# The state's update behind the 64-join, and decays, AH and X tied behind level copies, in the second DeltaNet pass of a diffusion step

## The chip, the cores and the metric

The kernel runs on one core of one Trainium2 chip. The metric is device time in microseconds (us) of one execution. The engines are named as in the profile: PE (TensorE, matmuls), DVE (VectorE), ACT (ScalarE), POOL (GpSimd) and SP (SyncE, which here only issues DMAs). A change of under 0.3% can't be told from none with this kernel.

## The reference

One layer of a hybrid backbone is run on 128 context tokens and 2048 latent tokens of width 1024, in float32. The token stream is normalised and modulated, projected once, and goes through two parallel groups of heads (a gated DeltaNet that is scanned in both directions, and a gated spatial MLP); their outputs are projected, added, and go through a squared-ReLU MLP. What matters here is the DeltaNet, cut to its core:

```python
a_mat = where(strict, einsum(k_beta, k) * decay, 0)          # per chunk and head
sol = triangular_solve(a_mat + eye, [v * beta, k_beta * exp(g)])
u, w = sol[..., :DV], sol[..., DV:]
qk = einsum(q, k) * decay
def step(S, xs):
    v_new = u_c - w_c @ S
    o = qd @ S + qk_c @ v_new
    S = S * exp(gl) + kd.T @ v_new
    return S, o
```

So every chunk needs a decay matrix, the inverse of a unit triangular matrix, and a step of a recurrent state S (4 heads of 128 x 128).

## The kernel before

The program has three stages. First come the projections, the convolution and the norms for 17 tiles of 128 tokens (one of context, sixteen latent). Then come the two DeltaNet passes, the first in the forward direction with the gated MLP as fill work, the second in the backward direction with the gating, the output projection w_out and the operands of the MLP as fill work. Then comes the MLP.

In the passes, a tile in one direction is a **unit**: units 0 to 16 are the forward pass (`d` is 0), units 17 to 33 the backward pass (`d` is 1, `NT` is 17). A unit has 17 **prep** steps that need no state and 4 **scan** steps that do. The prep steps, numbered from 0:

- 0: the decays. ACT makes `E` with four activations and one exponential (L1052, L1053), POOL masks it twice into `Es` and `E` (L1055, L1057).
- 1: DVE multiplies `KK` by beta and `Es`, one instruction per head (L1067); POOL sets the diagonal (L1071); ACT copies to f16 `AH` (L1074); DVE masks that into `X` (L1075).
- 2: PE transposes `X` (L1081), ACT copies `Y` (L1083), DVE makes the remainder `AL` (L1084).
- 3 to 12: the inverse, doubled in block size at levels 2, 4, 8, 16 and 32. Each level has two steps: PE multiplies `AH` and `Y` (L1101) and DVE masks the product into `P` (L1105); PE multiplies `P` and `X` twice (L1114, L1116) and ACT copies the new `Y` and `X` (L1117, L1118). At level 2 DVE also multiplies `QK` by `E` (L1121).
- 13 and 14: the **64-join**, the last doubling. Its first step is L1133 on PE and a copy `P` on ACT (L1134); its second is L1140 and L1142 on PE, a copy into `Y` on DVE (L1143) and one into `X` on ACT (L1144).
- 15 and 16: one Newton correction. PE multiplies `AH` and `AL` with `Y` (L1150, L1151), DVE makes `R` (L1153); PE multiplies `X` and `R`, ACT scales into `T` (L1162).

The scan steps: 0, the state times `kT` and `qT`; 1, `T` times `vt`, from which DVE makes `vs` (L1187) and ACT `vn` (L1189); 2, the **state's update**, eight f32 matmuls of `vs` and `kt` (L1026, `pd<-vs,kt`; an f32 product of a head shows as two) and four DVE instructions (L1201); 3, `QK` times `vn` and the output.

**The order of the work.** Every step gets a planned time in units of one period (one unit per period). With the second pass's figures (`WINDOWS`, from its ninth on), prep step j of unit n stands at n - 2.63 + (j + 0.5) * 2.57 / 17 and scan step j at n - 0.18 + (j + 0.5) * 1.18 / 4. While unit i is scanned, units i+1, i+2 and i+3 are in preparation. Fill work has times too: the eight w_out steps of a tile, of six matmuls each, are 0.125 apart (0.5975 and 0.7225 of a period are two of them), and a transpose stands at 0.5933. Steps are issued in the order of these times. A fill step is also bound on PE behind the first matmul of the fourth-last chain or prep step issued before it (`LAG3` is 3; `hist`).

A planner in the framework (`schedule_with_timeline_sim=True`) then makes the order of each engine from the order of issue: it runs a model of the engines and brings forward what it takes to be ready when an engine would be idle. On the chip each engine runs its list in order. A dependency added by `add_manual_dep` with `NoSync` puts no wait into the program; it only forbids the planner to place an instruction ahead of another one on the same engine.

`level_done` marks the last instruction of a step as urgent: the masks `P` of the levels on DVE and the copies `X` of the levels on ACT. `calm(f, lag)` issues `f` and binds each of its DVE and ACT instructions behind the last urgent one of its engine, or behind the one `lag` places further back. Before the change `calm` is used on the `KK` products of the second pass (lag 1), on one addition of the output projection (L1395) and on the steps that make the MLP's operands (L903, L904, L909).

Of the kernel before, what the change touches and what calls it, by code (L numbers as in the profile page):

```python
# [12 lines left out]
AF = mybir.ActivationFunctionType  # L13
ALU = mybir.AluOpType
# [7 lines left out]
NT = 17  # L22
NTOK = NT * P
H = 4
# [40 lines left out]
def hybrid_step(  # L65
# [7 lines left out]
    V, A, G, T = nc.vector, nc.scalar, nc.gpsimd, nc.tensor  # L73
# [74 lines left out]
    def bc4(ap):  # L148
        return ap.unsqueeze(1).to_broadcast([P, 4, P])
# [810 lines left out]
    with ExitStack() as ph:  # L960
# [41 lines left out]
        def level_done(n):  # L1002

            x = tc.nc.cur_bb.bb.instructions[-1]
            urgent[x.engine].append(x)

        def calm(f, lag=0):

            start = here()
            f()  # L1010
            for x in tc.nc.cur_bb.bb.instructions[start:]:
                if x.engine in urgent and len(urgent[x.engine]) > lag:
                    tc.add_manual_dep(x, urgent[x.engine][-1 - lag].name, mybir.DependencyInfo(
                        mybir.DependencyClass.NoSync, mybir.DependencyReason.DATA), reason="order")

        def unit(t, d):

            u = {}
            sg = 1 if d == 0 else -1

            def col(tab, h):
                return tab[:, t, d * 4 + h : d * 4 + h + 1]
# [25 lines left out]
            @prep.append  # L1048
            def _():
                e = s32("E")  # L1050
                for h in range(H):
                    A.activation(e[:, h, :], u["gb"][:, h, :], AF.Abs, scale=-1.0, bias=col(gcol, h))  # L1052
                A.activation(e, e, AF.Exp, scale=-1.0)  # L1053
                es = s32("Es")
                G.affine_select(out=es, in_=e, pattern=[[0, 4], [-sg, P]], compare_op=ALU.is_gt, fill=0.0,  # L1055
                                base=0, channel_multiplier=sg)
                G.affine_select(out=e, in_=e, pattern=[[0, 4], [sg, P]], compare_op=ALU.is_ge, fill=0.0,  # L1057
                                base=0, channel_multiplier=-sg)
                u["Es"], u["E"] = es, e

            @prep.append
            def _():
                a = u["KK"]

                def decayed():
                    for h in range(H):
                        V.scalar_tensor_tensor(out=a[:, h, :], in0=a[:, h, :], scalar=col(beta, h),  # L1067
                                               in1=u["Es"][:, h, :], op0=ALU.mult, op1=ALU.mult)

                calm(decayed, 1) if d else decayed()  # L1070
                G.affine_select(out=a, in_=a, pattern=[[0, 4], [1, P]], compare_op=ALU.not_equal, fill=1.0,  # L1071
                                base=0, channel_multiplier=-1)
                u["AH"], u["AL"], u["X"] = f16("AH", BA), f16("AL", BA), f16("X", BX)
                A.copy(u["AH"], a)  # L1074
                V.tensor_tensor(out=u["X"], in0=u["AH"], in1=bc4(bd2), op=ALU.mult)  # L1075

            @prep.append
            def _():
# [57 lines left out]
            @prep.append  # L1136
            def _():
                p = pd()
                for h in range(H):
                    T.matmul(p[:, h, 0:64], u["X"][:, h, :], pms[64][:, h, rb], start=True, stop=True)  # L1140
                for h in range(H):
                    T.matmul(p[:, h, 64:P], pms[64][:, h, :], u["X"][:, h, ra], start=True, stop=True)  # L1142
                V.tensor_copy(u["Y"][ra, :, rb], p[ra, :, 0:64])  # L1143
                A.copy(u["X"][rb, :, ra], p[rb, :, 64:P])  # L1144

            @prep.append
# [44 lines left out]
            @scan.append  # L1191
            def _():
                s = u["s"]
                p = pd()
                quad(p, u["kt"], u["vs"])
                sn = q32("S", 2)
                if s is None:
                    A.copy(sn, p)
                else:
                    for h in range(H):  # L1200
                        V.scalar_tensor_tensor(out=sn[:, h, :], in0=s[:, h, :], scalar=col(egl, h),  # L1201
                                               in1=p[:, h, :], op0=ALU.mult, op1=ALU.add)
                u["sn"] = sn

            @scan.append
# [205 lines left out]
        def at(time, fn, kind=None):  # L1411
            events.append((time, len(events), fn, kind))

        def spread(t0, t1, steps, kind):
            for j, st in enumerate(steps):
                at(t0 + (t1 - t0) * (j + 0.5) / len(steps), st, kind)

        def scan_step(i, f):
            def g():
                u = units[i]  # L1420
                if "s" not in u:
                    u["s"] = None if i in (0, NT) else units[i - 1]["sn"] if i not in (1, NT + 1) else u["s0"]
                f()
            return g
# [26 lines left out]
        for i, u in enumerate(units):  # L1451
            w = p2 if i <= NT else p3
            at(i - 3 if i > 1 else -12.1, lambda i=i, u=u: noted(("kk", i), u["prep_loads"]))
            at(i - 3 if i > 1 else -11.1, lambda i=i, u=u: after_weights(
                u["qk_load"], (("kk", 1),) if i < 2 else (), (mybir.EngineType.SP,)))
            at(i - 1, lambda i=i, u=u: after_weights(u["scan_loads"], LATER.get(i, ()), (mybir.EngineType.SP,)))
            u["prep"][:2] = [lambda i=i, f=f: after_weights(f, AHEAD_OF.get(i, ()), (mybir.EngineType.Activation,
                                                                                    mybir.EngineType.DVE))
                             for f in u["prep"][:2]]
            n = len(u["prep"])  # L1460
            for j, st in enumerate(u["prep"]):
                at(i - w[0] + (j + 0.5) * (w[0] - w[1]) / n if i or j > 9 else -11.6 if j < 2
                   else 0.2 * j - 8.15, st, "prep")
            spread(i + w[2], i + w[3], [scan_step(i, f) for f in u["scan"]], "chain")
            if i in (0, NT):
                at(i - 1, lambda i=i: state_load(i))
                at(i + w[2] + (w[3] - w[2]) * 0.7, lambda i=i: after(i))
            if i >= NT:
                at(i, lambda u=u: o_loads(u))
                first, second = o_steps(u)  # L1470
                spread(i + p3[4], i + p3[5], first, "fill")
                spread(i + p3[6], i + p3[7], second, "fill")
                if u["t"] > 8:
                    st = h2_steps(u["t"], pj, fraw, w512, fpart, fhalf, lambda u=u: u["x2"])
                    spread(i + p3[8], i + p3[9] + 0.2, st[:5], "fill")
                    spread(i + p3[9] + 0.2, i + p3[9] + 2.1, [lambda f=f: calm(f) for f in st[5:]], None)
# [620 lines left out]
```

## Time and profile before

| | us |
|---|---|
| median of three runs | 2576.61 |
| lowest, highest | 2570.27, 2578.84 |
| the profiled execution | 2574.76 |
| its span, first to last instruction | 2573.0 |
| first DeltaNet pass in the trace, about | 440 to 870 |
| second DeltaNet pass in the trace, about | 870 to 1222 |

The prediction shows rows of three kinds. A row of the **windows** view has the stretch (us from the span's start), its length, and the busy time of PE, of PE's weight loads, of DVE, ACT and POOL, each with the number of instructions in brackets; then the granted PE clock (1.00 is full), the DMA engines' busy share and GB/s. A row of the **waits** view reads: engine, tile and line that waited, the instruction that released it; the total in us, the number of times, the longest. A row of the **timeline** has the start and the length in us, the engine, the line, the operation, out<-in, the shape and the number of instructions merged; in square brackets stands the engine's idle time just before and what released it. Instructions of DVE and ACT that follow each other overlap in these records by a tenth of a microsecond or so, so the time one takes is read from the start of the next.

### The profile page before, as it was taken

The numbers are of one execution on the slowest core, as the hardware profiler recorded it, in microseconds if no ns is written. First come the engines' busy times: TensorE is split into PE (matmuls) and PEld (weight loads), VectorE is DVE, ScalarE is ACT, GpSimd is POOL, SyncE is SP. The second block draws the span as 40 slices with busy tenths as digits, with TensorE's granted clock in tenths as the row PEclk, the third lists the DMA queues.
The fourth block names the chain that finished last, engine by engine and source line by source line (L and its number), as shares of the span: only waits on it lengthen the run. The fifth ranks groups of instructions, "written<-read, shape, count | busy, mean of one in ns | idle before, by whom it ended". The sixth has DMA issues, their size and how long they took to land.

```text
span 2573.0 us, 44472 instructions
## 1 busy us (share of the span) xinstructions
PE 2536.3 (99%) x15268; PEld 2136.7 (83%) x15268; DVE 1830.8 (71%) x3790; ACT 1260.1 (49%) x3119; POOL 229.3 (9%) x448
## 2 busy tenths in 40 slices
PE   9999999999999999999999999999999999999998
PEld 5999999788888788778888888888888887888887
DVE  5867756776676878885678877777675556785875
ACT  4755556555555767763355544444342433243442
POOL 3112212211110111110000000000000000000000
PEclk9999999999999999999999999999999999999999
DMA  8977737744445657785867789665589979776673
GB/s 286 310 215 212 212 114 245 248 160 148 145 155 166 213 190 247 253 280 183 292 199 245 238 281 348 195 180 172 146 272 374 334 263 314 256 258 205 221 264 112
DMA packets 503912, 588.66 MB, mean 229 GB/s; under 512 B 36148, under 2 KB 298588, under 8 KB 500102
## 3 DMA queue, kind: packets, MB, share of 16 engines
q1 hardware_dynamic: 503686, 585.82, 69.7%
q8 instruction: 120, 1.97, 0.3%
q14 instruction: 106, 0.87, 0.1%
HBM read 406.01 MB, written 179.67 MB: 228 GB/s over the span
## 4 chain that ended last, share of the span: by engine, by line
PE 56%; DVE 3%; DMA 3%; ACT 1%; issue 1%; SPq 0%; POOL 0%; POOLq 0%; DVEq 0%; ACTq 0%
PE f L243 16%; PE f L241 16%; PE f L242 16%; PE pd L1026 2%; PE pj L241 1%; PE pj L242 1%; PE pj L243 1%; DMA QK<-qk_d 1%; DMA raw<-in_w_ff_dram 1%; DVE opL L904 0%; DMA kT<-kT_d 0%; DMA h_d<-ev 0%; DVE o L1358 0%; DVE KK L1067 0%; DMA zraw<-z_d 0%
## 5 line engine op out<-in xcount | busy, mean ns | idle before, releaser
L243 PE MATMUL f<-hop,zL 128*128 128x512 f32 (+1 forms) x976 | 377.0, 387 | 1.8 <-DVE zL L1551 1.8
L241 PE MATMUL f<-hop,zH 128*128 128x512 f32 (+1 forms) x976 | 376.9, 387 | 1.2 <-ACT zH L1557 1.2
L242 PE MATMUL f<-hop,zH 128*128 128x512 f32 (+1 forms) x976 | 376.7, 386 | 0.0
L241 PE MATMUL f<-hop,wH 128*128 128x512 f32 x896 | 349.7, 391 | 1.6 <-ACT p L1630 1.6
L242 PE MATMUL f<-hop,wH 128*128 128x512 f32 x896 | 348.7, 389 | 0.0
L243 PE MATMUL f<-hop,wL 128*128 128x512 f32 x896 | 347.3, 389 | 0.0
L1557 ACT CAST zH<-zraw 128x512 fp32r<-128x512 f32 x240 | 146.8, 620 | 295.6 <-DVE zraw L1551 84.2
L243 PEld LDWEIGHTS f<-hop,zL 128*128 128x128 f32 x976 | 183.6, 188 | 39.5 <-DVE zL L1551 3.0
L241 PEld LDWEIGHTS f<-hop,zH 128*128 128x128 f32 x976 | 183.7, 188 | 38.7 <-ACT zH L1557 1.6
L242 PEld LDWEIGHTS f<-hop,zH 128*128 128x128 f32 x976 | 183.7, 188 | 37.7 <-DVE hop L1551 0.3
L1551 DVE TENSOR_TENSOR zL<-zraw,zH 128x512 fp32r<-128x512 f32 x240 | 163.3, 689 | 68.8 <-ACT zH L1557 55.7
L241 PEld LDWEIGHTS f<-hop,wH 128*128 128x128 f32 x896 | 168.2, 188 | 37.3 <-ACT p L1630 3.1
L243 PEld LDWEIGHTS f<-hop,wL 128*128 128x128 f32 x896 | 168.2, 188 | 35.5
L242 PEld LDWEIGHTS f<-hop,wH 128*128 128x128 f32 x896 | 168.3, 188 | 34.6
L241 PE MATMUL pj<-kH,wH 128*128 128x386 f32 (+2 forms) x568 | 190.5, 338 | 1.8 <-ACT junk L601 1.1
L243 PE MATMUL pj<-kH,wL 128*128 128x386 f32 (+2 forms) x568 | 189.7, 335 | 0.0
L242 PE MATMUL pj<-kL,wH 128*128 128x386 f32 (+2 forms) x568 | 189.4, 335 | 0.0
L184 POOL TENSOR_TENSOR r<-rsq,nhalf 128x1 f32<-128x1 f32 (+1 forms) x37 | 23.0, 622 | 1398.1 <-DVE rsq L183 1398.1
L571 DVE SCALAR_TENSOR_TENSOR cv<-pj,vec,cv 128x384 f32<-128x384 f32 (+2 forms) x164 | 87.1, 540 | 53.3 <-ACT cv L568 52.0
L1557 ACT CAST wH<-s 128x512 fp32r<-128x512 f32 x96 | 59.4, 621 | 124.7 <-DVE s L1551 118.2
L241 PEld LDWEIGHTS pj<-kH,wH 128*128 128x128 f32 x568 | 107.1, 189 | 5.3 <-issue 2.1
L202 DVE TENSOR_TENSOR wL<-raw,wH 128x512 fp32r<-128x512 f32 x120 | 81.1, 685 | 38.8 <-ACT wH L201 38.6
(423 smaller groups left out, 5793.6 us busy)
## 6 DMA issues: line engine op xcount, KB each, us to landing
zraw<-z_d SPq DMA_DIRECT2D x212, 256.0 KB
raw<-in_w_ff_dram SPq DMA_DIRECT2D x192, 256.0 KB
hop<-hop_d SPq DMA_DIRECT2D x28, 1024.0 KB
z_d<-c SPq DMA_DIRECT2D x96, 256.0 KB
zraw<-s_d SPq DMA_DIRECT2D x96, 256.0 KB
raw<-in_w_mod_dram SPq DMA_DIRECT2D x80, 256.0 KB
r<-in_w_ff_dram SPq DMA_DIRECT2D x80, 256.0 KB
s_d<-s SPq DMA_DIRECT2D x64, 256.0 KB
```

What stands on the lines that cost most here:

```text
L184: G.tensor_tensor(out=out, in0=t[:np_, :n], in1=nhalf[:np_, :n], op=ALU.pow)
L202: V.tensor_tensor(out=lo, in0=raw, in1=f32(h), op=ALU.subtract)
L241: T.matmul(ps, lh, rh, start=first and i == 0, stop=False, skip_group_check=more)
L242: T.matmul(ps, lh, rl, start=False, stop=False, skip_group_check=more)
L243: T.matmul(ps, ll, rh, start=False, stop=last and i == n - 1, skip_group_check=more)
L571: V.scalar_tensor_tensor(out=cv[:, o : o + m], in0=ps[:, s + sh : s + sh + m], scalar=convw[:, w, j : j + 1], in1=cv[:, o : o + m], op0=AL ...
L1026: T.matmul(p[:, h, :], lhs[:, h, :], rhs[:, h, :], start=True, stop=True)
L1551: V.tensor_tensor(out=out, in0=a, in1=b, op=op)
L1557: A.copy(h, src)
```

## The change

All of it is in the two DeltaNet passes, and all of it but one mark acts in the second:

- the copy `Y` of the 64-join (L1143) is marked urgent, in both passes;
- scan step 2 of units 18 to 33 is issued 0.12 of a period later, at 0.6775 in place of 0.5575, and in the second pass its four DVE instructions are bound behind the last urgent DVE instruction;
- in the second pass the decays (prep step 0) are bound on ACT behind the third-last urgent copy, `AH` behind the last urgent copy on ACT, and `X` behind the last urgent instruction on DVE.

No instruction is added or taken away.

```diff
@@ -1048,9 +1048,13 @@
             @prep.append
             def _():
                 e = s32("E")
-                for h in range(H):
-                    A.activation(e[:, h, :], u["gb"][:, h, :], AF.Abs, scale=-1.0, bias=col(gcol, h))
-                A.activation(e, e, AF.Exp, scale=-1.0)
+
+                def decay():
+                    for h in range(H):
+                        A.activation(e[:, h, :], u["gb"][:, h, :], AF.Abs, scale=-1.0, bias=col(gcol, h))
+                    A.activation(e, e, AF.Exp, scale=-1.0)
+
+                calm(decay, 2) if d else decay()
                 es = s32("Es")
                 G.affine_select(out=es, in_=e, pattern=[[0, 4], [-sg, P]], compare_op=ALU.is_gt, fill=0.0,
                                 base=0, channel_multiplier=sg)
@@ -1071,8 +1075,12 @@
                 G.affine_select(out=a, in_=a, pattern=[[0, 4], [1, P]], compare_op=ALU.not_equal, fill=1.0,
                                 base=0, channel_multiplier=-1)
                 u["AH"], u["AL"], u["X"] = f16("AH", BA), f16("AL", BA), f16("X", BX)
-                A.copy(u["AH"], a)
-                V.tensor_tensor(out=u["X"], in0=u["AH"], in1=bc4(bd2), op=ALU.mult)
+
+                def parts():
+                    A.copy(u["AH"], a)
+                    V.tensor_tensor(out=u["X"], in0=u["AH"], in1=bc4(bd2), op=ALU.mult)
+
+                calm(parts) if d else parts()
 
             @prep.append
             def _():
@@ -1141,6 +1149,7 @@
                 for h in range(H):
                     T.matmul(p[:, h, 64:P], pms[64][:, h, :], u["X"][:, h, ra], start=True, stop=True)
                 V.tensor_copy(u["Y"][ra, :, rb], p[ra, :, 0:64])
+                level_done(64)
                 A.copy(u["X"][rb, :, ra], p[rb, :, 64:P])
 
             @prep.append
@@ -1197,9 +1206,13 @@
                 if s is None:
                     A.copy(sn, p)
                 else:
-                    for h in range(H):
-                        V.scalar_tensor_tensor(out=sn[:, h, :], in0=s[:, h, :], scalar=col(egl, h),
-                                               in1=p[:, h, :], op0=ALU.mult, op1=ALU.add)
+
+                    def update():
+                        for h in range(H):
+                            V.scalar_tensor_tensor(out=sn[:, h, :], in0=s[:, h, :], scalar=col(egl, h),
+                                                   in1=p[:, h, :], op0=ALU.mult, op1=ALU.add)
+
+                    calm(update) if d else update()
                 u["sn"] = sn
 
             @scan.append
@@ -1461,7 +1474,9 @@
             for j, st in enumerate(u["prep"]):
                 at(i - w[0] + (j + 0.5) * (w[0] - w[1]) / n if i or j > 9 else -11.6 if j < 2
                    else 0.2 * j - 8.15, st, "prep")
-            spread(i + w[2], i + w[3], [scan_step(i, f) for f in u["scan"]], "chain")
+            for j, f in enumerate(u["scan"]):
+                behind_join = 0.12 if j == 2 and i > NT else 0.0
+                at(i + w[2] + (w[3] - w[2]) * (j + 0.5) / 4 + behind_join, scan_step(i, f), "chain")
             if i in (0, NT):
                 at(i - 1, lambda i=i: state_load(i))
                 at(i + w[2] + (w[3] - w[2]) * 0.7, lambda i=i: after(i))
```

## The prediction

> **What bounds the kernel now.** I read the page's first part, then the busy time of the two DeltaNet passes, then what TensorE (PE) waited for in the second pass, where the whole edit lies.
>
> ```profile
> PE 2536.3 (99%) x15268; PEld 2136.7 (83%) x15268; DVE 1830.8 (71%) x3790; ACT 1260.1 (49%) x3119; POOL 229.3 (9%) x448
> ...
> 440.00:870.00 430.00, 424.67 (x3618) 352.52 (x3617) 306.40 (x852) 235.91 (x637) 63.62 (x81) 1.00 0.55 179
> 870.00:1222.00 352.00, 337.40 (x2954) 281.03 (x2953) 279.51 (x707) 226.26 (x709) 50.37 (x63) 1.00 0.68 228
> ...
> PE pd L1150 <- DVE Y L1143: 4.9, 7, 1.9
> PE pd L1101 <- ACT Y L1117: 4.2, 7, 1.3
> PE pd L1133 <- ACT Y L1117: 2.0, 4, 0.9
> PE pd L1026 <- ACT X L1118: 1.4, 1, 1.4
> PE pd L1026 <- DVE rsq L183: 1.1, 1, 1.1
> PE pd L1114 <- DVE P L1105: 0.6, 1, 0.6
> PE pd L1140 <- ACT P L1134: 0.2, 1, 0.2
> ```
>
> PE bounds the program: it is busy for 99% of the span. The first pass leaves it idle for 430.00 - 424.67 = 5.3 us, the second for 352.00 - 337.40 = 14.6 us, and the seven rows at the end (us in total, times, longest) hold 14.4 of those 14.6. The matmuls are the same before and after, so these 14.6 us, and what they draw after them, are all there is to win: 0.6% of the time. VectorE (DVE) is busy for 279.51 of the 352 us and ScalarE (ACT) for 226.26; both run in order, and each wait stands behind something on one of them.
>
> **The clock's share.** The longest wait has a tail.
>
> ```profile
> 1157.05 1.12 DVE L1201 SCALAR_TENSOR_TENSOR S<-S,egl,pd 128x128 f32<-128x128 f32 x4
> 1158.19 0.43 DVE L1143 CAST Y<-pd 64x256 f16<-64x256 f32 x1
> 1158.77 0.22 PE L1150 MATMUL pd<-Y,AH 128*128 128x128 f16 x1 [1.86 <-DVE Y L1143]
> ...
> 1160.00:1162.00 2.00, 2.00 (x10) 1.65 (x10) 1.13 (x3) 0.66 (x4) 0.00 (x0) 0.50 0.75 260
> 1162.00:1164.00 2.00, 2.00 (x13) 1.38 (x12) 0.10 (x1) 0.95 (x6) 0.00 (x0) 0.66 0.34 103
> ```
>
> After the 1.86 us the granted clock (the figure behind the five busy times) falls to 0.50 and 0.66: 2 x (0.50 + 0.34) = 1.7 us of PE's work lost. I charge these to the wait, so they go with it. The Trainium skill (TensorE: Matmul & The Clock Gate, "HAM oscillation — how this bites in real kernels") asks only that no PE-idle gap exceed some 3.4 us; by that rule 1.86 us would be harmless, the 1.7 us would have another cause and stay, and the saving below would be 4.8 us in place of 6.5. The trace speaks against it here: the drop follows the pass's longest wait, and I keep the row.
>
> **The update behind the join's copy.** In the rows above, the state's update (four DVE instructions, 1.12 us) stands right ahead of the copy Y that L1150 waits for. So it does in six of the seven waits; at the seventh, the shortest, the copy itself waits for its matmuls. Two things now move it back. The new tie puts the four behind the copy: 1.1 us less. And the step is issued at 0.6775 of the period instead of 0.5575, past the join's second step (0.562), the second step of level 8 of the next unit but one (0.655), the KK step of the unit after that (0.597), and, among the fill work, one w_out step and one transpose. The step issues eight matmuls and four DVE instructions, no DMA, and nothing to SP's or POOL's queue.
>
> ```profile
> 1131.13 1.14 PE L1026 MATMUL pd<-vs,kt 128*128 128x128 f32 x8
> 1132.03 0.48 PE L241 MATMUL pj<-wH,oH 128*128 128x512 f32 x1
> ...
> 1134.41 1.12 DVE L1201 SCALAR_TENSOR_TENSOR S<-S,egl,pd 128x128 f32<-128x128 f32 x4
> 1139.68 1.14 PE L1026 MATMUL pd<-S,kT 128*128 128x128 f32 x8
> ```
>
> The eight matmuls take 1132.03 - 1131.13 = 0.90 us, ahead of the join's second step now, between it and L1150 then. So the copy has 1.1 + 0.9 = 2.0 us more, above the longest wait: **4.9 us and the 1.7 us of clock go**. The next reader of S is the next unit's product S,kT, which starts 1139.68 - 1135.53 = 4.2 us after the update's end; a delay of some 2 us is covered there, so S costs nothing. If the cover were gone the price would be that delay.
>
> **What the eight matmuls covered.** They stood between the join's first step (L1133) and its second (L1140), while ACT makes P at L1134.
>
> ```profile
> 889.23 0.38 ACT L1134 ACTIVATE P<-pd 64x256 f16<-64x256 f32 x1
> 890.52 0.22 PE L1140 MATMUL pd<-P,X 128*128 128x64 f16 x2
> ...
> 997.27 0.38 ACT L1134 ACTIVATE P<-pd 64x256 f16<-64x256 f32 x1
> 997.70 0.28 PE L1140 MATMUL pd<-P,X 128*128 128x64 f16 x4 [0.21 <-ACT P L1134]
> ...
> 1153.55 0.38 ACT L1134 ACTIVATE P<-pd 64x256 f16<-64x256 f32 x1
> 1154.57 0.28 PE L1140 MATMUL pd<-P,X 128*128 128x64 f16 x4
> ```
>
> From P's end to L1140 passes at least 0.05 us (the middle pair, which waits). Over the thirteen periods from the first pair to the last the distance is 0.91, 0.20, 0.68, 1.12, 0.37, 0.05, 1.32, 0.96, 0.55, 0.87, 1.32, 0.86 and 0.64; take 0.05 off each and see what 0.90 is short of: 0.04 + 0.75 + 0.27 + 0.58 + 0.90 + 0.40 + 0.08 + 0.09 + 0.31 = **3.4 us of new waits** if nothing else fills the hole, 0 if the planner puts a fill step there. I take all of it, since the same shift also holds the fill step of 0.7225 back behind L1140 (its fourth-last chain or prep step is now the join).
>
> **Decays, AH and X.** AH's copy now comes behind the X copy of level 4, and KK's four products are held back too, by no line of the diff of their own: their tie is to the last mark but one on DVE, and with the join's copy marked that is level 8's mask instead of level 4's.
>
> ```profile
> 1127.83 1.13 DVE L1067 SCALAR_TENSOR_TENSOR KK<-KK,beta,Es 128x128 f32<-128x128 f32 x4
> 1129.59 0.59 ACT L1189 COPY vn<-pd 128x512 f32<-128x512 f32 x1 [1.15 <-DVE vs L1187]
> 1130.07 0.62 ACT L1074 CAST AH<-KK 128x512 f16<-128x512 f32 x1
> 1130.59 0.38 ACT L1117 CAST Y<-pd 128x256 f16<-128x256 f32 x1
> 1130.73 0.43 DVE L1075 TENSOR_TENSOR X<-AH,bd 128x512 f16<-128x512 f16 x1 [0.57 <-ACT AH L1074]
> 1131.02 0.28 PE L1101 MATMUL pd<-Y,AH 128*128 128x64 f16 x4 [1.28 <-ACT Y L1117]
> ...
> 910.61 0.28 PE L1133 MATMUL pd<-Y,AH 128*128 128x64 f16 x4 [0.94 <-ACT Y L1117]
> 1085.35 0.28 PE L1101 MATMUL pd<-Y,AH 128*128 128x64 f16 x4 [0.80 <-ACT Y L1117]
> ```
>
> AH takes 1130.59 - 1130.07 = 0.52 us of ACT just ahead of the Y that L1101 waits for, and the copy vn ahead of AH waits for vs, which stood behind KK's 1.13 us. Both leave: 1.6 us, more than the 1.28. The waits of 0.94 and 0.80 have the same row of instructions ahead of them. **3.0 us go.** The decays' tie, to the third-last copy, takes E, which the planner runs well before it is used, out of a stretch like this:
>
> ```profile
> 1063.68 1.28 ACT L1052 ACTIVATE E<-gb,gcol 128x128 f32<-128x128 f32 x4
> 1067.51 0.63 ACT L1053 ACTIVATE E<-E 128x512 f32<-128x512 f32 x1
> 1068.72 1.16 PE L1026 MATMUL pd<-vn,QK 128*128 128x128 f32 x8 [1.35 <-ACT X L1118]
> ```
>
> Without the five E instructions (some 1.7 us of ACT) X comes early enough: **1.4 us go**. E then runs ahead of its KK with a few us to spare; POOL's two selections and the QK product wait for it. The wait of 1.1 us put down to rsq I leave as it is: it may hang on R's reading of a PSUM bank, which stays; 0 to 1.1, I take 0. The other rows of the first fence (some 4 us) have T, the gelu or a mask ahead of them and stay.
>
> KK's new place costs something that the rows of before do not show, since PE's order is made anew.
>
> ```profile
> 911.97 0.42 DVE L1105 TENSOR_TENSOR P<-pd,sm 128x256 f16<-128x256 f32 x1
> 914.11 0.39 PE L1081 MATMUL pd<-ident,X 128*128 128x128 f16 x4
> ...
> 1152.78 0.41 DVE L1105 TENSOR_TENSOR P<-pd,sm 128x256 f16<-128x256 f32 x1
> 1156.51 0.40 PE L1081 MATMUL pd<-ident,X 128*128 128x128 f16 x4
> ```
>
> KK to X's end takes 1131.16 - 1127.83 = 3.3 us, now counted from that mask; L1081, which transposes X, starts 1.72 us after it in the first pair and 3.32 us in the last. At PE's old order the twelve periods from the first to the last would be short of 1.61 + 1.44 + 1.58 + 2.02 + 0.76 + 0 + 0 + 1.98 + 0.85 + 0 + 0.56 + 0.01 = 10.8 us. But L1081 is no fixed place: in the first pair it follows the level's matmuls at once, in the last a group of w_out matmuls is ahead of it, so the planner sets it by when it believes X ready. So 0 to 10.8; nearest is the wait that such planned masks left, 0.6 us once in the pass, and I take twice that, 1.1.
>
> **The sum**, against the profiled execution (2574.76 us, span 2573.0): -4.9 - 1.7 - 3.0 - 1.4 + 3.4 + 1.1 = **-6.5 us, 2568.3**. That execution lies 1.85 below the median of the three runs (2576.61), so for a median **2570.1**, 0.25% less. A measurement of this kernel can tell about 0.3%, 7.7 us, from no change: the forecast ends just inside.
>
> **Rivals.**
> 1. *The waits change hands* (2573.4). The update's part works, -6.6, L1140's new wait costs its 3.4, and the ACT waits only move to other copies, since ACT has the same work. For it: the seven waits for Y at L1101 have different neighbours each time. Against it: three of them show AH and KK plainly.
> 2. *Slower: X late at its transpose* (2588). If PE's order leaves L1081 less than 3.3 us behind level 8's mask, the 10.8 us are paid, with the two waits above 1.86 us halving the clock for 1.7 us each: -11.0 + 3.4 + 10.8 + 3.4 = +6.6, 2583. AH also falls behind two copies of some 0.25 us each, so 3.8 us for the chain: 15.9 us short, five waits above 1.86: +17, 2594. I name the middle. Against it: the differing places of L1081.
> 3. *Nearly all waits go* (2562). Of 14.6 + 1.7 = 16.3 us some 14 go, because the planner fills the hole at L1140. For it: the first pass, with the same chain and fill work, leaves 5.3 us in a longer stretch.
> 4. *It does nothing* (2576.6): the planner already took these orders in most periods, and small shifts elsewhere eat the rest. Against it: the update is ahead of the copy in six waits.
>
> **How the numbers follow.** Forecast 0.40, rival 1 0.23, rival 2 0.15, rival 3 0.15, rival 4 0.07. The forecast's own range is -2 to -12 us, 2564.5 to 2574.5: only L1150's share with L1140's costs, or no costs and the 1.1 of rsq gained. For 8 in 10 I take 2560 to 2583, which leaves out most of rival 2 and the outer edge of rival 3. Faster by over 0.3% (under 2568.9): under half of the forecast's 0.40, all of rival 3, a little of rival 1: 0.36. Slower (over 2584.3): most of rival 2, and something for unnamed shifts: 0.17. Within: 0.47.
>
> **What would show it.** In the second pass of the changed kernel: no row L1150 <- Y, and the copy L1143 ahead of the update in every period; no clock below 1.00 near the pass's end; L1101 <- Y down to about 1 us; a new row L1140 <- P of up to 3.4 us; L1081 with little or no wait for X; PE idle of 9 to 10 us in place of 14.6. A row L1081 <- X of several us, or masks late behind the KK products, would prove rival 2. I am wrong if PE's idle time falls and the span does not, or if L1150 still waits.

## The result, and the profile after

| | before | after | ratio, with its 95% interval |
|---|---|---|---|
| timed together first (6 runs each), us | 2576.94 | 2561.86 | 0.9951 [0.9936, 0.9965] |
| timed together last (11 and 7 runs), us | 2571.62 | 2563.47 | 0.9968 [0.9957, 0.9979] |
| span of the profiled execution, us | 2573.0 | 2559.5 | |

The change makes the kernel faster, by 0.3 to 0.5%. The changed kernel came out alike both times; the kernel before stood at 2577 in the first comparison and at 2572 in all later ones, so the 15 us of the first comparison are too much. The last one gives 8; e6 and e8 below, which run the second pass in the same order as the changed kernel or nearly so, gave 10 and 11 against a kernel before of 2572.

From the profile after: the first part of the page, the two passes in the windows view, and what PE waited for in the second pass (total, times, longest). The columns are those of the first fence of the prediction.

```profile
PE 2531.2 (99%) x15268; PEld 2135.2 (83%) x15268; DVE 1829.7 (71%) x3790; ACT 1258.6 (49%) x3119; POOL 228.2 (9%) x448
...
440.00:870.00 430.00, 424.91 (x3622) 352.77 (x3621) 306.57 (x856) 233.17 (x632) 61.69 (x79) 1.00 0.55 178
870.00:1222.00 352.00, 343.82 (x2995) 287.35 (x2995) 284.51 (x715) 231.49 (x719) 51.88 (x66) 1.00 0.68 230
...
PE pd L1141 <- ACT Y L1125: 2.2, 2, 1.4
PE pd L1109 <- ACT Y L1125: 1.8, 3, 0.8
PE pj L241 <- DVE tmp L1407: 1.6, 2, 0.8
PE pd L1159 <- DVE Y L1151: 0.6, 1, 0.6
PE pm L1384 <- DVE ug L1264: 0.5, 1, 0.5
PE pm L241 <- DVE tmp L1407: 0.4, 2, 0.2
PE pd L1122 <- DVE vt L1183: 0.4, 1, 0.4
PE pd L1026 <- DVE o L1233: 0.2, 1, 0.2
PE pd L1148 <- ACT P L1142: 0.2, 1, 0.2
```

The lines have moved: the levels' first step L1101 is L1109 now, the join's steps L1133 and L1140 are L1141 and L1148, the Newton product L1150 is L1159, the join's copy L1143 is L1151, `KK` L1067 is L1071, `vs` and `vn` are L1196 and L1198, the update L1201 is L1212. In the same 352 us PE is idle for 8.2 us in place of 14.6. The wait for the join's copy fell from 4.9 to 0.6, the levels' and the join's waits for ACT's `Y` from 6.2 to 4.0, and the two waits of `vn,QK` and of `rsq` (1.4 and 1.1) are gone; what w_out waits for `tmp` grew from 0.2 to 2.0. Each of these rows is of one execution. A second execution of each order is e1 (for before) and e12 (for after), both below. In e1 the join's copy has 4.8 us, ACT's `Y` 6.6, `tmp` 0.5 and the masks `P` 3.0, where before has 0.6; in e12 they have 0.6, 1.8, 1.8 and 0.9, where after has no row of `P`. So a single row can move by some 2 us with no edit.

A fixed window holds different work in two kernels. The pass is therefore measured between two landmarks too, from ACT's copy of the pass's first state to the first matmul of the MLP. First before, then after:

```profile
869.80:1237.40 367.60, 353.00 (x3026) 293.99 (x3025) 292.36 (x728) 230.53 (x716) 50.37 (x63) 1.00 0.67 223
```

```profile
869.50:1228.60 359.10, 350.92 (x3027) 293.04 (x3026) 291.02 (x727) 233.84 (x722) 52.34 (x66) 1.00 0.68 230
```

The pass is 8.5 us shorter: 14.6 - 8.2 = 6.4 of idle PE, and 2.1 of PE's busy time. The 1.7 us of halved clock lie in the busy time, but so does more: e1 below has the order of before and no drop in the pass, and is busy for 352.06, and e5 for 354.67 without a drop. The 8.5 us are about the gain of the last comparison. The spans differ by 13.5; of the other 5.0 us 4.7 lie in the MLP, from its first matmul to the end (2573.0 - 1237.4 = 1335.6 before, 2559.5 - 1228.6 = 1330.9 after). There the profile before had this (timeline, and the window after it):

```profile
2185.88 0.50 PE L243 MATMUL f<-hop,zL 128*128 128x512 f32 x1 [1.76 <-DVE zL L1551]
...
2188.00:2190.00 2.00, 2.00 (x7) 1.51 (x6) 2.00 (x4) 0.68 (x2) 0.00 (x0) 0.50 0.92 306
```

The changed kernel's profile has no such wait. Neither has a kernel with all five parts switched off (e1 below), whose MLP takes 2572.5 - 1239.5 = 1333.0; the changed kernel's second profile (e12) takes 2557.7 - 1225.5 = 1332.2. So this belonged to one execution of the kernel before, and not to the change.

What stands behind the waits that went is seen in the timeline of the changed kernel (start, length, engine, operation; in brackets the idle time and its releaser):

```profile
1058.26 0.68 DVE L1196 TENSOR_TENSOR vs<-pd,eglg 128x512 f32<-128x512 f32 x1
1058.86 1.12 DVE L1071 SCALAR_TENSOR_TENSOR KK<-KK,beta,Es 128x128 f32<-128x128 f32 x4
...
1058.97 0.59 ACT L1198 COPY vn<-pd 128x512 f32<-128x512 f32 x1 [2.92 <-DVE vs L1196]
1059.93 0.39 ACT L1125 CAST Y<-pd 128x256 f16<-128x256 f32 x1
...
1061.42 0.50 PE L241 MATMUL pm<-wH,oH 128*128 128x512 f32 x1 [0.18 <-DVE tmp L1407]
...
1062.68 0.40 PE L243 MATMUL pm<-wH,oL 128*128 128x512 f32 x1
...
1062.69 0.38 ACT L1142 ACTIVATE P<-pd 64x256 f16<-64x256 f32 x1
...
1063.12 0.28 PE L1148 MATMUL pd<-P,X 128*128 128x64 f16 x4
1063.35 1.14 PE L1026 MATMUL pd<-vs,kt 128*128 128x128 f32 x8
...
1064.88 0.43 DVE L1151 CAST Y<-pd 64x256 f16<-64x256 f32 x1
1066.13 1.12 DVE L1212 SCALAR_TENSOR_TENSOR S<-S,egl,pd 128x128 f32<-128x128 f32 x4
1066.72 0.23 PE L1159 MATMUL pd<-Y,AH 128*128 128x128 f16 x1
```

Two pairs on DVE have changed places. The join's copy (1064.88) is ahead of the update (1066.13); before, the update was ahead. And `vs` (1058.26) is ahead of the four `KK` products (1058.86); before, `KK` at 1127.83 in the prediction's rows was ahead of this `vs`:

```profile
1128.88 0.68 DVE L1187 TENSOR_TENSOR vs<-pd,eglg 128x512 f32<-128x512 f32 x1
```

The copy `vn` on ACT, with the level's `Y` behind it, waited for `vs`. The first swap was predicted. The second was not, and the experiments show that the gain needs it.

### The profile page after: what moved, and what is told of

Read it like the earlier page. It is cut to its first block, busy times and chain, and to the rows that moved or that the text cites. A ratio compares the mean times of both kernels' runs of the same rounds, so it can differ in the third digit from the quotient of the medians.

```text
span 2559.5 us, 44412 instructions
## 1 busy us (share of the span) xinstructions
PE 2531.2 (99%) x15268; PEld 2135.2 (83%) x15268; DVE 1829.7 (71%) x3790; ACT 1258.6 (49%) x3119; POOL 228.2 (9%) x448
## 3 DMA queue, kind: packets, MB, share of 16 engines
q8 instruction: 120, 1.97, 0.3%
## 4 chain that ended last, share of the span: by engine, by line
PE 88%; DMA 5%; DVE 4%; ACT 2%; issue 1%; SPq 0%; POOL 0%; POOLq 0%; DVEq 0%; ACTq 0%
PE f L241 16%; PE f L243 16%; PE f L242 16%; PE pj L241 7%; PE pj L243 7%; PE pj L242 7%; PE pd L1026 5%; PE pm L241 2%; PE pm L243 1%; PE pm L242 1%; PE pt L625 1%; DMA raw<-in_w_mod_dram 1%; PE pt L584 1%; DMA QK<-qk_d 1%; DMA raw<-in_w_ff_dram 1%
```

## The experiments

Every kernel below computes everything. Diffs are against the changed kernel. For each I counted, over the pass's periods, which of the two pairs on DVE comes first. In every kernel the answer is one-sided, but for the pass's first period, in which `vs` is ahead of `KK` in all of them.

| kernel | update / join's copy | `KK` / `vs` | ratio to before, 95% | pass, us | PE idle in it |
|---|---|---|---|---|---|
| before | update first | `KK` first | 1 | 367.6 | 14.6 |
| e1, all parts off | update | `KK` | 1.0002 [0.9993, 1.0011] | 369.9 | 17.8 |
| e4, mark alone | update | `KK` | 0.9982 [0.9973, 0.9992] | 365.3 | 11.9 |
| e2, update's part alone | copy | `KK` | 1.0013 [1.0004, 1.0022] | 371.8 | 17.6 |
| e5, decay tie off | copy | `KK` | 1.0006 [0.9997, 1.0016] | 370.9 | 16.2 |
| e3, ties of decays, AH, X alone | update | `vs` | 0.9978 [0.9968, 0.9988] | 365.8 | 13.2 |
| e7, no shift | update | `vs` | 0.9977 [0.9966, 0.9988] | 365.9 | 13.0 |
| e6, AH and X tie off | copy | `vs` | 0.9953 [0.9938, 0.9968] | 357.8 | 6.9 |
| e8, `KK` tied less | copy | `vs` | 0.9955 [0.9940, 0.9970] | 360.8 | 9.0 |
| e9, decays free, `KK` behind `vs` | copy | `vs` | 0.9975 [0.9964, 0.9986] | 361.7 | 8.0 |
| e10, `vs` marked too | copy | `vs` | 0.9966 [0.9955, 0.9978] | 362.2 | 10.4 |
| e11, shift and decay tie alone | copy | `vs` | 0.9962 [0.9949, 0.9975] | 359.6 | 7.5 |
| after, first profile | copy | `vs` | 0.9951 [0.9936, 0.9965] | 359.1 | 8.2 |
| e12, the changed kernel again | copy | `vs` | 0.9968 [0.9957, 0.9979] | 357.8 | 6.9 |

PE idle is the pass less PE's busy time. Two executions of one order differ by 1.3 and 2.3 us in the pass (367.6 and 369.9; 359.1 and 357.8), and e8, which has the changed kernel's order in the pass, adds 360.8; so a pass alone tells apart no less than 3.0 us. e1 to e4 were timed together, e5 to e8, e9 to e11, and e12 alone, each with the kernel before.

**e1_base: all five parts off.** This is the kernel before in the changed kernel's text, and in its trace the order of every engine is that of before.

```diff
-                calm(decay, 2) if d else decay()
+                decay()
...
-                calm(parts) if d else parts()
+                parts()
...
-                level_done(64)
+                pass
...
-                    calm(update) if d else update()
+                    update()
...
-                behind_join = 0.12 if j == 2 and i > NT else 0.0
+                behind_join = 0.0 if j == 2 and i > NT else 0.0
```

> The changed text with all five of its parts switched off (no mark, no ties, no shift): the program of before on the changed text's line numbers. It computes everything. Both theories expect the time of before, 2577 us within 0.3%, and the second pass's PE idle time near 14.6 us with the longest wait followed by a drop of the clock. It tells whether the 1.8 us wait of PE at about 2186 us, in the MLP's second stage, which the changed kernel does not have, belongs to the program of before (theory A: it comes back here, so 3 to 5 us of the gain lie in the MLP and follow from the pass's different end) or is an accident of one execution (theory B: it is gone or stands elsewhere).

It measures as the kernel before, 1.0002. It also shows how much of a profile is chance. Here are the pass and the clock after its longest wait (timeline, then windows):

```profile
869.60:1239.50 369.90, 352.06 (x3026) 293.07 (x3026) 292.67 (x728) 230.29 (x716) 50.40 (x63) 1.00 0.66 222
...
1161.32 0.22 PE L1159 MATMUL pd<-Y,AH 128*128 128x128 f16 x1 [1.88 <-DVE Y L1151]
...
1162.00:1164.00 2.00, 2.00 (x17) 1.82 (x17) 1.68 (x3) 0.37 (x2) 0.00 (x0) 1.00 0.78 242
1164.00:1166.00 2.00, 2.00 (x18) 1.66 (x18) 0.00 (x0) 1.24 (x7) 0.00 (x0) 1.00 0.51 154
```

The wait that the prediction charged with 1.7 us of clock is here again, 1.88 us long, and the clock stays at 1.00; both theories had expected a drop.

**e2_update and e3_ties: one half of the change each.** e2 keeps the shift, the mark and the update's tie; e3 keeps the ties of the decays, of `AH` and of `X`.

```diff
 e2
-                calm(decay, 2) if d else decay()
+                decay()
...
-                calm(parts) if d else parts()
+                parts()
 e3
-                level_done(64)
+                pass
...
-                    calm(update) if d else update()
+                    update()
...
-                behind_join = 0.12 if j == 2 and i > NT else 0.0
+                behind_join = 0.0 if j == 2 and i > NT else 0.0
```

> The update's part alone: the shift by 0.12, the mark on the join's copy and the tie of the four update instructions; decays, AH and X free. KK is held back too, through the mark. By my prediction's terms 4.9 + 1.7 us go and up to 3.4 us come at L1148 (the join's second step): about 2573, and the waits of the level's first step for Y stay near 4 us. Rival: the mark and its hold on KK carry the gain, then 2565 or less, with the waits for Y gone as well.

> The other half alone: decays, AH and X tied, no mark, no shift, no tie of the update. By my terms the waits for Y with AH ahead of them go, but KK is not held back, so at most 3.0 + 1.4 us go: about 2573, and the waits for the join's copy stay near 4.9 us with the drop of the clock. Rival: the ties alone do most of it, 2566 or less.

e2 is not faster than before (0.13% slower, 2575.02 us where 2573 was expected), although the update is behind the join's copy in every period. Its pass and its longest rows of waits:

```profile
866.50:1238.30 371.80, 354.19 (x3027) 296.69 (x3026) 293.70 (x728) 229.88 (x716) 50.71 (x63) 1.00 0.66 220
...
PE pd L1141 <- ACT Y L1125: 5.6, 5, 1.3
PE pm L241 <- DVE tmp L1407: 3.5, 4, 1.3
PE pd L1109 <- ACT Y L1125: 3.1, 5, 1.3
PE pj L241 <- DVE tmp L1407: 1.9, 3, 0.6
PE pd L1122 <- DVE P L1113: 1.5, 4, 0.7
PE pd L1148 <- ACT P L1142: 1.1, 3, 0.6
```

The row L1159 <- Y is gone, as the swap should make it, and others have grown in its place: the join's first step waits 5.6 us for ACT's `Y` (2.0 before, 2.9 in e1) and w_out 5.4 for `tmp` (0.2 before, 0.5 in e1). e3 gains 0.22%, about what was expected of it, with the update still ahead of the copy, and the wait for the copy grows:

```profile
PE pd L1159 <- DVE Y L1151: 7.1, 11, 1.3
```

So neither half is the change: their effects add up to -0.1%, the whole brings -0.3 to -0.5%.

**e4_mark: the mark alone.** e2's edit without the shift and the update's tie.

```diff
-                calm(decay, 2) if d else decay()
+                decay()
...
-                calm(parts) if d else parts()
+                parts()
...
-                    calm(update) if d else update()
+                    update()
...
-                behind_join = 0.12 if j == 2 and i > NT else 0.0
+                behind_join = 0.0 if j == 2 and i > NT else 0.0
```

> Only the mark on the join's copy: the additions and subtractions of the output projection and of the MLP's operands that were tied to the last mark now stand behind this copy, and KK behind level 8's mask; the update, the decays, AH and X are as before. If being held behind the copy is what counts, the waits for the join's copy fall from 4.9 to under 2 us although the update still stands ahead of it, and the time is 2570 or less; by my terms the update's 1.1 us stay ahead of the copy, most of the 4.9 us stays, and KK's later place costs up to 10.8 us at X's transpose (L1089): 2575 to 2588.

One line gives 0.18%, where the prediction's terms had the mark alone at 2575 to 2588, and takes most of the wait for the join's copy with neither pair swapped:

```profile
PE pd L1159 <- DVE Y L1151: 1.1, 3, 0.6
```

The mark can act through the fill instructions that `calm` binds behind the last urgent one; which of them it was is not shown. So the two pairs of the table do not account for every difference: e4, with neither swapped, gains about as much as e3 with one. The mark does not add to the rest: with the ties (e7 beside e3) it brings nothing, and e11, which lacks it, has the whole gain.

**e5_no_decay: the whole change without the decay tie.**

```diff
-                calm(decay, 2) if d else decay()
+                decay()
```

> The changed kernel with the decays free again on ACT. The two halves alone gave a second pass 2 to 4 us longer (the update's) and 2 to 4 us shorter (the ties'), the whole some 10 us shorter, so the parts need each other. Theory A (what stands ahead of the level copies on ACT decides once the update is out of the way): the waits for ACT's Y come back, 2 to 4 us, and the time is 0.1 to 0.2% above the changed kernel. Theory B (the decays have slack anywhere, AH and X carry the ties' half): within 0.1% of the changed kernel.

The whole gain goes, 1.0006, more than either theory expected. By the prediction this line was worth 1.4 us; by this run the whole gain hangs on it. Its pass, two of its waits, and from its timeline an `E` and the next `KK` and `vs`:

```profile
868.90:1239.80 370.90, 354.67 (x3026) 293.44 (x3025) 294.34 (x728) 230.64 (x716) 52.36 (x63) 1.00 0.66 221
...
PE pm L241 <- DVE tmp L1407: 3.6, 3, 1.7
PE pd L1122 <- DVE P L1113: 3.6, 5, 1.2
...
1046.94 1.28 ACT L1054 ACTIVATE E<-gb,gcol 128x128 f32<-128x128 f32 x4
...
1062.08 1.14 DVE L1071 SCALAR_TENSOR_TENSOR KK<-KK,beta,Es 128x128 f32<-128x128 f32 x4
...
1063.74 0.69 DVE L1196 TENSOR_TENSOR vs<-pd,eglg 128x512 f32<-128x512 f32 x1
```

Most of the waits that came back are for DVE (masks, `tmp`), though the tie is on ACT. And `KK` is back ahead of `vs`, in every period but the first. That gave the theory that the later runs test: the tie's use is the order on DVE, not the room on ACT.

**e6_no_parts: AH and X not tied. e8_kk_free: KK tied to the third-last mark.**

```diff
 e6
-                calm(parts) if d else parts()
+                parts()
 e8
-                calm(decayed, 1) if d else decayed()
+                calm(decayed, 2) if d else decayed()
```

> The changed kernel with AH and X free again; KK is still held behind level 8's mask through the mark. Theory A (AH right ahead of Y): the waits of the level's first step for Y come back, 3 to 4 us, 0.15% above the changed kernel. Theory B (it is KK's later place that freed these waits, and AH follows KK by itself): within 0.1% of it.

> The changed kernel with the KK products tied one mark further back (third-last), which is where they stood before the mark was added. Theory A (KK's later place, which no line of the change names, is what takes vs and the copy vn out of the way of ACT's Y): the waits for Y rise by 2 to 3 us, 0.1% above the changed kernel. Theory B (KK's place does not matter, or costs at X's transpose): the same within 0.1%, or faster.

Both measure as the change itself does, 0.9953 and 0.9955. The AH and X tie does nothing that can be measured: without it the traces have the same order on PE and ACT, and within the pass 10 pairs of DVE instructions in another order. e8 is no test of where `KK` should stand. By the spacing worked out in the next section it ties `KK` to level 32's mask, further back than before the change, and in its trace PE, DVE and ACT run the whole pass in the changed kernel's order; so that tie does not bind there, and e8 is one more timing of the same pass.

**e7_no_shift.**

```diff
-                behind_join = 0.12 if j == 2 and i > NT else 0.0
+                behind_join = 0.0 if j == 2 and i > NT else 0.0
```

> The changed kernel with the update issued at its old time; its tie then binds it to level 8's mask, since the join's copy is marked only later, so it can stand ahead of the copy again. Theory A (the shift is needed): waits of L1159 for the copy come back, 3 to 5 us, 0.15 to 0.2% above the changed kernel. Theory B (the mark alone moves enough other DVE work behind the copy): L1159's waits stay near 1 us as with the mark alone, and since the eight matmuls go on covering the join's copy P, the time is at the changed kernel's or below.

Without the shift the update is ahead of the copy again in spite of its tie (issued earlier, it is tied to an earlier mark), and the ratio is 0.9977, against 0.9953 and 0.9955 for e6 and e8 in the same comparison, as theory A had it:

```profile
PE pd L1109 <- ACT Y L1125: 6.1, 7, 2.0
PE pd L1159 <- DVE Y L1151: 2.9, 4, 1.7
```

The shift without the update's tie was not run by itself. In e11 below the update is shifted and not tied, and the copy is ahead of it in every period; in e3, with the ties of decays, AH and X and no shift, it is not. So the shift makes that swap without the tie.

**e9_kk_behind_vs: the test of the theory.** The decays are as free as in e5, and each `KK` product is forbidden to stand ahead of the last `vs` issued before it.

```diff
+        vs_of = []
...
-                calm(decay, 2) if d else decay()
+                decay()
...
+                start = here()
...
+                for x in tc.nc.cur_bb.bb.instructions[start:]:
+                    if d and vs_of and x.engine == mybir.EngineType.DVE:
+                        tc.add_manual_dep(x, vs_of[-1].name, mybir.DependencyInfo(
+                            mybir.DependencyClass.NoSync, mybir.DependencyReason.DATA), reason="order")
...
+                vs_of.append(tc.nc.cur_bb.bb.instructions[-1])
```

> The changed kernel with the decays free on ACT, as in the run without the decays' tie (ratio 1.0006), but with the KK products of a unit bound on DVE behind the vs product that is issued before them. So far two orders on DVE sort all the runs: the update ahead of or behind the join's copy, and KK ahead of or behind vs. Theory A (the decays' tie works only through DVE: with Es later the planner puts vs ahead of KK): the gain comes back, 0.994 to 0.997 of before, and the waits for ACT's Y and DVE's masks fall. Theory B (what counts is that the decays no longer stand among the level copies on ACT): it stays within 0.1% of 1.0006.

```profile
868.00:1229.70 361.70, 353.75 (x3028) 293.51 (x3027) 294.23 (x728) 230.93 (x716) 52.74 (x63) 1.00 0.67 226
...
PE pd L1115 <- ACT Y L1131: 2.3, 4, 1.0
PE pd L1147 <- ACT Y L1131: 1.6, 3, 0.9
```

The pass is 361.7 against e5's 370.9 and the changed kernel's 359.1 and 357.8, and the ratio 0.9975 against 1.0006 and 0.9968, just above theory A's 0.994 to 0.997 and clear of theory B. (L1115 and L1147 are the levels' and the join's first step here.) So most of what the decay tie brings comes back with one tie between `KK` and `vs`, with `E` free on ACT. The tie moved more than this pair, since the planner makes every order anew: within the pass 176 pairs of DVE instructions swapped between e5 and e9, 52 of them a `KK` and a `vs`, and 243 pairs on ACT and 816 on PE. What those others add is not shown. The intervals of e9 and of the changed kernel (e12) overlap, so whether a rest is left to `E`'s own place stays open.

**e10_vs_mark: `vs` marked urgent as well.**

```diff
                 V.tensor_tensor(out=u["vs"], in0=p, in1=cols, op=ALU.mult)
+                if d:
+                    level_done(0)
```

> The changed kernel with one mark more: vs is urgent too in the second pass, so that what is tied to the last mark on DVE (the additions of the output projection, the MLP operands' subtractions) stands behind vs as well, and KK behind vs by a tie. In the changed kernel the copy vn still waits on ACT for vs and holds Y up behind it. Theory A (vs is the instruction that the second pass waits for on DVE): the waits for Y, 4.0 us, fall to 1 to 2 us, 0.1% below the changed kernel, 0.994 of before. Theory B (the rest is spread over other causes): the same as the changed kernel within 0.1%.

No gain beyond the change, 0.9966, with a pass of 362.2, as theory B had it. The levels' and the join's waits for `Y` are 2.3 us (4.0 and 1.8 in the changed kernel's two profiles), and one row has grown:

```profile
PE pd L1148 <- ACT P L1142: 5.3, 4, 1.9
...
1018.25 0.28 PE L1148 MATMUL pd<-P,X 128*128 128x64 f16 x4 [1.88 <-ACT P L1142]
1063.71 0.28 PE L1148 MATMUL pd<-P,X 128*128 128x64 f16 x4 [1.85 <-ACT P L1142]
```

This is the wait that the prediction feared at the join's second step. It exists, at 5.3 us, in this order and not in the changed kernel's.

**e11_decay_shift: the shift and the decay tie alone**, without mark, update tie, AH and X tie.

```diff
-                calm(parts) if d else parts()
+                parts()
...
-                level_done(64)
+                pass
...
-                    calm(update) if d else update()
+                    update()
```

> Two of the five parts: the shift of the update and the decays' tie, without the mark, the update's tie and the ties of AH and X. Both orders on DVE are those of the changed kernel. Theory A (the two orders decide): 0.995 to 0.996 of before. Theory B (the mark's hold on the other tied DVE work adds its own part, as the mark alone gave 0.9982): 0.997 of before.

0.9962, a pass of 359.6: two of the five parts, the shift and the decay tie, make both swaps and bring the whole gain within what can be told (the ratio lies between the two theories). No version clearly beats the changed kernel.

**e12_after_again: the changed kernel once more**, with no edit, to settle how large the gain is.

> The changed kernel itself once more, as the control for the runs above: before stood at 2577 us when the change was first timed and at 2572 us in every comparison since. It tells how much of the changed kernel's first 0.9951 is the change, and how far KK behind vs alone (0.9975) is from it. Theory A (the first ratio holds): 0.994 to 0.996, so the decays' place on ACT is worth 0.2% beside the order of KK and vs. Theory B (part of the first ratio was the moment of timing): 0.996 to 0.997, and the order on DVE is all but the whole of the decays' share. In the trace: the second pass near 359 us from the first state's copy to the MLP's first matmul again, and the MLP's second stage without or with a wait near 1.8 us by chance.

0.9968 [0.9957, 0.9979], the pass at 357.8: the second line of the result's table.

## Why the prediction was right and wrong

The forecast was 2570.1 and the range 2560 to 2583; 2561.86 lies inside, at its lower edge. The forecast's change of -6.5 us is near the -8.2 of the last comparison and under half of the first one's -15.1. A gain above 0.3% had a chance of 0.36 there, no change 0.47. The sign has its cause only in part where the prediction put it, and that the sum came near is partly luck: 4.5 us of costs that never came stood against gains counted too high and new waits that it did not have.

By its terms, from the rows of waits in the 352 us of the pass, one execution of each kernel:

| term | predicted | measured |
|---|---|---|
| wait for the join's copy | -4.9 | 0.6 - 4.9 = -4.3 |
| clock | -1.7 | -1.7 |
| `Y` at the levels' and the join's first step | -3.0 | 4.0 - 6.2 = -2.2 |
| `vn,QK` | -1.4 | -1.4 |
| join's second step for `P` | +3.4 | 0.0 |
| transpose for `X` | +1.1 | 0.0 |
| `rsq`, mask `P` | 0 | -1.1 - 0.6 = -1.7 |
| `tmp`, and new rows `ug`, `vt`, `o` | 0 | 1.6 + 0.4 - 0.2 + 0.5 + 0.4 + 0.2 = +2.9 |
| sum | -6.5 | -8.4 |

- **The update behind the join's copy: right in place, and no gain by itself.** L1159 <- Y went from 4.9 us in seven waits to 0.6 in one, and the copy is first in every period. But e2, which does this alone, is slower than before: what stood behind these waits on the path took their place. The step that failed is to subtract a wait's whole length, for it assumes that nothing else is nearly as late. In e2 something was: ACT's `Y` and `tmp`.
- **AH, KK and E: the wrong lines.** The step said 3.0 us go at L1101 and L1133 since `AH` and `KK` leave, and 1.4 at `vn,QK` since `E` leaves ACT. Measured: 2.2 of 6.2, and 1.4. But e6 shows that the AH tie brings nothing: `AH` leaves its place ahead of `Y` without it. And the `vn,QK` row is gone in e2, e4 and e5 too, where `E` is as free as before, so its going does not show that the reason given was right. What made the difference is seen in the rows of before: `vn` waits for `vs`, `vs` stands behind `KK`, and `Y` behind `vn`. The decay tie swaps `vs` and `KK` on DVE, and e5 and e9 show that most of its gain comes with this swap. Why the planner does so when `E` comes later (with `Es`, which `KK` reads, ready later in its model) is argued and not shown.
- **Why `KK` did not move back: an error in the spacing.** The prediction and the text on the kernel before it took the prep steps of the second pass to be 2.57 / 17 of a period apart. `WINDOWS` has 2.63 and -0.06, so it is (2.63 + 0.06) / 17 = 0.158. The join's second step then stands at 0.664, not 0.562, and `KK` at 0.607, ahead of it: when `KK` is issued the join's copy is not yet marked, and its tie is the old one. Level 8's second step stands at 0.715, so the shift does not pass it; nor does the fill step of 0.7225 go behind the join, for the fourth-last chain or prep step with matmuls ahead of it is level 8's first either way. The claim of `KK` behind level 8's mask fell with it, and so did rival 2, whose 10.8 us rested on that mask: no row L1089 <- X (L1081 before) appears in the pass.
- **L1140's new waits: +3.4 predicted, none measured.** The row L1148 <- P is 0.2 us as it was (0.6 in e12). In the timeline after, w_out matmuls stand ahead of the join's second step, from 1061.42 until the one at 1062.68, while ACT makes `P`. The bound of 0 was the right end. e10 shows that it hangs on the planner's order: 5.3 us there.
- **X at its transpose: +1.1 predicted, none measured**, for the reason given above.
- **The clock: 1.7 us that the wait did not own.** They are gone after, but e1 has the same wait with no drop, so this part of the sum was luck. The term should have been a chance; the last section says on what it seems to hang.
- **Rival 3 had the time** (2562) and one half of the reason, that the planner fills the hole at L1148. The other half, that 14 of the 16.3 us go, is wrong: 6.4 of idle PE and 1.7 of clock went. Its time was met in the first comparison because the kernel before stood some 5 us higher there than in all later comparisons.
- **Rivals 1 and 4** did not happen here; rival 1, the waits changing hands, is what e2 and e5 do.

Of the 8.2 us of idle PE that are left 7.9 lie in nine rows, the largest of 2.2 us.

## What to carry to other kernels

Where engines run in order and a planner makes the order, a tie is worth what it does to the order of other pairs: compare the orders of before and after on every engine, count pairs that swapped, and only then read which wait each swap should move. A removed wait brings its length only if the next operand is in time; here one swap alone lost a little, the other alone won half, and both together won more than the sum. Plan times used in an argument are to be worked out from the code's own numbers, signs included: one sign here moved a step by a tenth of a period and undid three statements.

## What the runs showed of the hardware

Waits of PE of the same length are sometimes followed by a halved clock and sometimes not. One window behind the first of e10's two waits quoted above, and two behind the second:

```profile
1020.00:1022.00 2.00, 2.00 (x11) 1.60 (x10) 1.91 (x4) 1.90 (x5) 0.00 (x0) 1.00 0.57 182
...
1064.00:1066.00 2.00, 2.00 (x17) 2.00 (x14) 2.00 (x5) 1.20 (x4) 0.00 (x0) 0.68 0.41 156
1066.00:1068.00 2.00, 2.00 (x6) 1.60 (x6) 1.91 (x6) 1.82 (x5) 0.00 (x0) 0.50 0.80 270
```

After 1.88 us of waiting at 1018.25 the clock stays at 1.00; after 1.85 us at 1063.71 it falls to 0.50. Between 100 and 2550 us the fourteen traces have ten waits of PE of 1.7 us or more. Four of them (1.97 in e7, 1.86 and 1.76 before, 1.85 in e10) were followed by a drop, and six (two of 1.88, and 1.79, 1.78, 1.75 and 1.71) were not, so length does not decide. A fifth drop, in e2, followed two waits of 1.25 and 0.64 us that are 1.5 us apart.

Where a wait falls seems to decide. In each trace the clock changes only at multiples of 3.41 us from its first change, and each of the five drops lasts one such step at 0.50, which is 1.7 us of PE's work. In the step just before each of the five drops PE was idle for 1.76 to 1.97 us. The wait of 1.88 us in e1 is cut by the edge of a step into 0.31 and 1.57, and e10's at 1018.25 into 0.58 and 1.30. Over all fourteen traces no step with up to 1.68 us of idle time was followed by a drop, and of the six steps with 1.76 or more five were; the sixth, in e7, had 1.79. So by these traces a wait costs the clock when it leaves PE idle for about half of one step, and where the steps lie differs from one execution to the next.

The Trainium skill (TensorE: Matmul & The Clock Gate, "What's actually happening") says that activity is judged in a free-running window of 3413 ns. The steps of 3.41 us in these traces agree with it. The rule "no PE-idle gaps >~3.4µs" of the Trainium skill (TensorE: Matmul & The Clock Gate, "HAM oscillation — how this bites in real kernels") is too wide as a safe limit here: 1.76 us was enough.
